# A fused two-layer block: half of the tokens' experts by gathered rows, half dense, in place of a quarter and three quarters

## The chip, the cores and the metric

One Trainium2 chip, one core. The metric is the device time of one execution in microseconds (us). The kernel before was timed three times: 2209.03, 2210.12 and 2216.78, so its median is 2210.12.

## The reference, cut to what matters

The program runs two transformer layers on 512 tokens of width 1024. The change touches the second half of the first layer, a product-key expert layer with 16384 experts of one row each:

```python
def block(xb):                                  # 128 tokens, width 1024
    q = (xb @ w_query).reshape(128, 8, 2, 128)
    s = einsum('chpd,hpnd->chpn', q, sub_keys)  # 8 heads, 2 halves, 128 keys
    top_s, top_i = top_k(s, 16)
    cand = top_s[:, :, 0, :, None] + top_s[:, :, 1, None, :]
    best_s, pos = top_k(cand, 16)               # 16 experts for each head
    idx = take(top_i[..0..] * 128 + top_i[..1..], pos)
    g = softmax(best_s)
    act = gelu(einsum('cd,chkd->chk', xb, expert_u[idx]))
    return einsum('chk,chkd->cd', g * act, expert_v[idx])
```

Each token thus uses 8 x 16 = 128 rows of `expert_u` and 128 rows of `expert_v`, of 4 KB each. Attention and a norm come before; the final norm, another attention and a dense feed-forward layer come behind.

## The kernel before, in words

All products on TensorE are done as three matmuls of split operands (`mm3`, lines 198 to 201): every weight tile is loaded by SP (line 93), copied to a rounded high part by ACT (line 111), and the low part is subtracted by VectorE, or by GpSimd where the stream says `lo=G` (line 112). `Stream` keeps 4 raw tiles of 128x512 in flight and 5 split ones.

The expert layer is done in two ways at once.

**Gathered:** for token block 0 (128 tokens on 128 partitions) the 128 chosen rows of `u` and the 128 of `v` are fetched by indirect DMAs from GpSimd's queue, one expert slot of all 128 tokens, 128 rows of 4 KB, at a time (`gather`, lines 1065 to 1078). VectorE forms each dot product with `hn` (line 1070), and adds each weighted `v` row to `acc` (line 1078). The row tiles are three (line 976), used in turn by `u` and `v`.

**Dense:** for blocks 1 to 3 (TD = 384 tokens) all 16384 experts are computed, 128 experts at a time: `u_side(b)` (24 matmuls of 384 columns, line 1029), gelu, a multiplication with the gates of the 128 experts (`weigh`), and `v_side` (3 token blocks x 2 halves x 3 matmuls of 512 columns into six PSUM banks, line 1055). The gate of every (expert, token) pair is built from the chosen indices by one-hot tiles on VectorE and matmuls on TensorE (`gate_hot`, `gate_sum`) for groups of 8 tokens, in three chunks of 38, 45 and 45 experts-rows, into a ring of 60 slots.

The order is: `query`, `level1`, `level2` for the 8 heads with all four blocks together (lines 939 to 948; the top-k runs on VectorE, with candidate sums and index selects partly on GpSimd); then the first chunk of gates (48 groups, lines 1096 to 1102); then the loop over the 128 dense expert blocks (lines 1115 to 1130), in which the other two chunks of gates are built in two stretches of blocks, and gathered units are handed out by a planned share for each block (`share`, `scale`, `due`). After block 120 the gathered block is finished with the residual and the final norm (lines 1132 to 1144); behind the loop the same is done for the other three blocks (lines 1179 to 1190).

GpSimd issues its instructions in order, so a gather that waits for a free row tile holds back the low parts and index selects that stand behind it; VectorE and TensorE are in order too. The order on an engine is made by the framework from priorities, and `issue_after` pins it.

Of the kernel before, what the change touches and what calls it, by code (L numbers as in the profile page):

```python
# [9 lines left out]
FT = mybir.dt.float32  # L10
# [10 lines left out]
P = 128  # L21
# [11 lines left out]
TD = S - P  # L33
CH = (38, 45, 45)
CW = max(CH)
RING = 60
# [11 lines left out]
RB = 1  # L48
ADA_E = 8
# [108 lines left out]
def body(ctx, tc, a):  # L158
# [622 lines left out]
    hA = pk.tile([P, 2, KD, S], FR, name="hA")  # L781
    hD = hA[:, :, :, P:]
    h0 = hA[:, :, :, :P]
    late["h0"] = h0
    hn = pk.tile([P, D], FT, name="hn")
    gw0 = pk.tile([P, P], FT, name="gw0")
    idx = pk.tile([P, P], I32, name="idx")
    iT = pk.tile([P, 2, TD], F16, name="iT", tag="iT")
    gp = pk.tile([P, TD, 2], F16, name="gp", tag="gp")
    ioth = pk.tile([P, P, 4], F16, name="ioth")  # L790
    with ExitStack() as s2:
        pn = pool(s2, "pn", 2)

        def norm2(b):
# [66 lines left out]
    def level1(m, top, tif):  # L861
        q = m % 2
# [11 lines left out]
        sc = pb.tile([P, NB, P], FT, name=f"scs{m}", tag="scs", bufs=2)  # L874
        A.activation(sc, p2, AF.Copy)
        ti = pb.tile([P, NB, 16], U32, name=f"tpi{m}", tag="tpi")
        for b in range(NB):
            V.max(out=top[:, b, q, 0:8], in_=sc[:, b])
            V.max_index(out=ti[:, b, 0:8], in_max=top[:, b, q, 0:8], in_values=sc[:, b])
            V.match_replace(out=sc[:, b], in_to_replace=top[:, b, q, 0:8], in_values=sc[:, b], imm_value=LOWEST)  # L880
            V.max(out=top[:, b, q, 8:16], in_=sc[:, b])
            V.max_index(out=ti[:, b, 8:16], in_max=top[:, b, q, 8:16], in_values=sc[:, b])
        A.activation(tif[:, :, q], ti, AF.Copy)

    def level2(h, top, tif):

        sh = [P, NB, 16]
        cand = pb.tile([P, NB, 80], FT, name=f"cand{h}", tag="cand")
        G.tensor_tensor(cand[:, :, 0:16], top[:, :, 0, 0:1].to_broadcast([P, NB, 16]), top[:, :, 1, :], op=OP.add)
        G.tensor_tensor(cand[:, :, 16:72].rearrange("p b (u w) -> p b u w", w=8),  # L890
                        top[:, :, 0, 1:8, None].to_broadcast([P, NB, 7, 8]),
                        top[:, :, 1, None, 0:8].to_broadcast([P, NB, 7, 8]), op=OP.add)
        G.tensor_tensor(cand[:, :, 72:80], top[:, :, 0, 8:16], top[:, :, 1, 0:1].to_broadcast([P, NB, 8]), op=OP.add)
        best = pb.tile([P, NB, 16], FT, name=f"best{h}", tag="best")
        pos = pb.tile([P, NB, 16], U32, name=f"pos{h}", tag="pos")
        for b in range(NB):
            V.max(out=best[:, b, 0:8], in_=cand[:, b])
            V.max_index(out=pos[:, b, 0:8], in_max=best[:, b, 0:8], in_values=cand[:, b])
            V.match_replace(out=cand[:, b], in_to_replace=best[:, b, 0:8], in_values=cand[:, b], imm_value=LOWEST)
            V.max(out=best[:, b, 8:16], in_=cand[:, b])  # L900
            V.max_index(out=pos[:, b, 8:16], in_max=best[:, b, 8:16], in_values=cand[:, b])
        ge = pb.tile([P, NB, 16], FT, name=f"ge{h}", tag="ge")
        V.tensor_tensor(ge, best, best[:, :, 0:1].to_broadcast(sh), op=OP.subtract)
        last["exp"] = A.activation(ge, ge, AF.Exp).ins

        i0 = pb.tile(sh, I32, name=f"i0{h}", tag="i0")
        V.tensor_scalar(i0, pos, 8.0, 0.0, op0=OP.subtract, op1=OP.max)
        ex = pb.tile(sh, FT, name=f"ex{h}", tag="ex")
        V.tensor_scalar(ex, pos, 72.0, 0.0, op0=OP.subtract, op1=OP.max)
        t1 = pb.tile(sh, FT, name=f"t1{h}", tag="t1")  # L910
        V.tensor_scalar(t1, pos, 16.0, -8.0, op0=OP.is_ge, op1=OP.mult)
        V.tensor_scalar(i0, i0, 3, None, op0=OP.arith_shift_right)
        V.tensor_add(t1, t1, pos)
        wi = pb.tile([P, 2, NB, 16], F16, name=f"wi{h}", tag="wi")
        V.tensor_add(wi[:, 0], i0, ex)
        V.scalar_tensor_tensor(t1, i0, -8.0, t1, op0=OP.mult, op1=OP.add)
        V.tensor_sub(wi[:, 1], t1, ex)
        hs = slice(h * 16, (h + 1) * 16)
        for q in range(2):

            for k0, n in ((0, 8), (8, 16)):
                eq = pb.tile([P, NB, 16, 8], F16, name=f"eq{h}_{q}_{k0}", tag="eq", bufs=5)[:, :, :n]
                V.tensor_tensor(eq, wi[:, q, :, None, k0:k0 + 8].to_broadcast([P, NB, n, 8]),
                                iotk[:, None, 0:n].to_broadcast([P, NB, n, 8]), op=OP.is_equal)
                G.tensor_tensor(eq, eq, tif[:, :, q, 0:n, None].to_broadcast([P, NB, n, 8]), op=OP.mult)
                eqs.append((ix[:, q, :, h * 16 + k0:h * 16 + k0 + 8], eq.rearrange("p b n k -> p b k n")))
        gs = pb.tile([P, NB], FT, name=f"gs{h}", tag="gs")
# [646 lines left out]
```

## Time and profile before

| | |
|---|---|
| runs, median (lowest, highest) | 2210.12 us (2209.03, 2216.78) |
| profiled execution, own time | 2222.11 us |
| its span | 2220.3 us |
| TensorE (PE) busy | 2102.8 us, 95% |
| VectorE (DVE) busy | 1624.1 us, 73% |
| ScalarE (ACT) busy | 954.2 us, 43% |
| GpSimd (POOL) busy | 618.3 us, 28% |
| DMA moved | 375.79 MB, 169 GB/s over the span |
| of which gathered rows' queue | 134.23 MB |

The span is that of the program on the core; the own time adds what lies around it. Matmuls overlap each other in the records, so a busy PE is not PE at its peak: the step from one matmul's start to the next tells its cost. Stretches of the span that belong to a stage are read with the view of windows: busy time of each engine in a stretch, then the granted clock as a share of full speed, the busy share of the 16 DMA engines and the GB/s moved.

### The profile page before, as it was taken

Reading aid. Unit: us, or ns where it says so; the run is one execution under the profiler, and the core shown is the slowest. Engines: PE = TensorE matmul, PEld = TensorE weight load, DVE = VectorE, ACT = ScalarE, POOL = GpSimd, SP = SyncE. Lnnn points to the kernel's source line nnn. Section 1 sums busy time; section 2 is a strip of 40 time slices with the busy share of each in tenths; the row PEclk is TensorE's granted clock in tenths of the full one; section 3 lists DMA queues with packets and bytes.
Section 4 is the critical chain, followed back from the end, with each engine's and each line's share of the span. In section 5 each row is a group of like instructions: output and inputs, shape, how many; then the busy total and the mean of one; then the engine's idle time right before and its main releaser. Section 6 shows DMA issues by size and latency. Waiting matters only on the chain.

```text
span 2220.3 us, 35038 instructions
## 1 busy us (share of the span) xinstructions
PE 2102.8 (95%) x12443; PEld 1771.4 (80%) x12443; DVE 1624.1 (73%) x3587; ACT 954.2 (43%) x1899; POOL 618.3 (28%) x553
## 2 busy tenths in 40 slices
PE   7999998888999999999999999999998999999999
PEld 5756787778888888888888888788887678888887
DVE  7779889997878997777799777777767865333322
ACT  4467342345435553333355433333353553333321
POOL 2245245564222113333312233333303420000000
PEclk9999999988999999999999999999999999999999
DMA  8515522231575558878855688888844221333332
GB/s 273 166 49 164 173 70 66 89 111 57 172 254 191 168 166 270 281 268 285 285 186 165 196 279 268 262 265 281 295 138 122 65 67 45 98 96 99 95 117 73
DMA packets 163634, 375.79 MB, mean 169 GB/s; under 512 B 18562, under 2 KB 22530, under 8 KB 163459
## 3 DMA queue, kind: packets, MB, share of 16 engines
q1 hardware_dynamic: 121058, 233.81, 31.6%
q0 software_dynamic: 36864, 134.23, 19.3%
q10 hardware_dynamic: 5536, 5.51, 0.9%
q8 instruction: 98, 1.61, 0.3%
q14 instruction: 78, 0.63, 0.1%
HBM read 366.66 MB, written 4.19 MB: 167 GB/s over the span
## 4 chain that ended last, share of the span: by engine, by line
PE 56%; DVE 16%; DMA 15%; issue 6%; ACT 4%; POOL 2%; ACTq 0%; SPq 0%; DVEq 0%; POOLq 0%
DMA vr<-in_v_dram,idx 7%; PE vac L200 4%; PE vac L201 4%; PE vac L199 4%; PE pA L199 4%; PE pA L200 4%; PE pA L201 3%; DMA wr<-in_uT_dram 3%; DMA ur<-in_u_dram,idx 3%; PE pd L201 2%; PE pd L200 2%; PE pd L199 2%; PE upp L201 2%; PE upp L199 2%; PE upp L200 2%
## 5 line engine op out<-in xcount | busy, mean ns | idle before, releaser
L111 ACT ACTIVATE wh<-wr 128x512 fp32r<-128x512 f32 x716 | 446.8, 631 | 760.4 <-DMA wr<-in_v_dram 162.1
L112 DVE TENSOR_TENSOR wl<-wr,wh 128x512 fp32r<-128x512 f32 x640 | 429.4, 695 | 286.4 <-ACT wh L111 270.2
L200 PE MATMUL vac<-wl,wwh 128*128 128x512 f32 x756 | 305.4, 404 | 32.7 <-DVE wl L112 32.3
L199 PE MATMUL pA<-hA,wh 128*128 128x384 f32 x928 | 318.1, 343 | 0.0
L201 PE MATMUL pA<-hA,wl 128*128 128x384 f32 x928 | 314.7, 339 | 0.0
L200 PE MATMUL pA<-hA,wh 128*128 128x384 f32 x928 | 313.9, 338 | 0.0
L199 PE MATMUL vac<-wh,wwh 128*128 128x512 f32 x756 | 304.3, 403 | 0.7 <-ACT wwh L1042 0.5
L201 PE MATMUL vac<-wh,wwl 128*128 128x512 f32 x756 | 299.5, 396 | 0.1
L1067 POOL DMA_INDIRECT ur<-in_u_dram,idx x128 | 160.5, 1254 | 383.3 <-DVE acc L1078 308.2
L1067 POOL DMA_INDIRECT vr<-in_v_dram,idx x128 | 155.3, 1213 | 338.2 <-DVE ur L1070 252.5
L200 PEld LDWEIGHTS vac<-wl,wwh 128*128 128x128 f32 x756 | 144.2, 191 | 73.5 <-DVE wl L112 49.2
L1078 DVE SCALAR_TENSOR_TENSOR acc<-vr,act,acc 128x1024 f32<-128x1024 f32 x127 | 162.7, 1281 | 46.7 <-DMA vr<-in_v_dram,idx 45.4
L1070 DVE SCALAR_TENSOR_TENSOR ur<-ur,hn 128x1024 f32<-128x1024 f32 x128 | 156.2, 1220 | 39.0 <-DMA ur<-in_u_dram,idx 39.0
L199 PEld LDWEIGHTS pA<-hA,wh 128*128 128x128 f32 x928 | 177.0, 191 | 4.1 <-ACT ga L1031 0.7
L200 PEld LDWEIGHTS pA<-hA,wh 128*128 128x128 f32 x928 | 177.0, 191 | 3.1
L201 PEld LDWEIGHTS pA<-hA,wl 128*128 128x128 f32 x928 | 176.6, 190 | 0.0
L201 PEld LDWEIGHTS vac<-wh,wwl 128*128 128x128 f32 x756 | 144.0, 190 | 30.1 <-DVE wwl L1043 0.8
L199 PEld LDWEIGHTS vac<-wh,wwh 128*128 128x128 f32 x756 | 144.1, 191 | 28.7 <-ACT wh L111 0.9
L112 POOL TENSOR_TENSOR wl<-wr,wh 128x512 fp32r<-128x512 f32 x76 | 101.9, 1352 | 74.6 <-ACT wh L111 71.7
L1042 ACT ACTIVATE wwh<-w 128x384 fp32r<-128x384 f32 x126 | 66.0, 524 | 117.2 <-DVE w L1035 115.0
L1008 PEld LDWEIGHTS <-oj 128*128 128x128 f16 x1152 | 83.2, 117 | 38.1 <-issue 16.4
L989 DVE TENSOR_TENSOR oj<-iT,ioth 128x1024 f16<-128x1024 f16 x144 | 106.0, 740 | 9.2 <-PE pG L1009 9.2
(697 smaller groups left out, 4319.7 us busy)
## 6 DMA issues: line engine op xcount, KB each, us to landing
wr<-in_uT_dram SPq DMA_DIRECT2D x256, 256.0 KB
wr<-in_v_dram SPq DMA_DIRECT2D x256, 256.0 KB
wa<-in_w_adaT_dram SPq DMA_DIRECT2D x48, 512.0 KB
wr<-in_w_gate_dram SPq DMA_DIRECT2D x44, 256.0 KB
wr<-in_w_up_dram SPq DMA_DIRECT2D x44, 256.0 KB
wr<-in_w_down_dram SPq DMA_DIRECT2D x44, 256.0 KB
wr<-in_w_in_dram SPq DMA_DIRECT2D x36, 256.0 KB
wr<-in_w_out_dram SPq DMA_DIRECT2D x32, 256.0 KB
```

The lines of the kernel that those rows point to most:

```text
L111: self.nc.scalar.activation(hi, raw, AF.Copy)
L112: (lo_eng or self.nc.vector).tensor_tensor(lo, raw, hi.bitcast(FT), op=OP.subtract)
L199: T.matmul(out, lh, rh, start=start, stop=False)
L200: T.matmul(out, lh, rl, start=False, stop=False)
L201: return T.matmul(out, ll, rh, start=False, stop=stop).ins
L989: V.tensor_tensor(out, iT[:, q, tt].rearrange("p (s t) -> p s t", t=4)[:, :, None].to_broadcast([P, GS // 4, w, 4]), ioth[:, None, j0:j0 + ...
L1008: T.matmul(pt[:, t, :n], oj[:, t // 4, :, t % 4], o[:, :, 1], start=True, stop=False)
L1042: A.activation(wh, w, AF.Copy)
L1067: G.indirect_dma_start(out=r, out_offset=None, in_=a[kind], in_offset=bass.IndirectOffsetOnAxis(ap=idx[:, j:j + 1], axis=0))
L1070: V.scalar_tensor_tensor(r, r, 1.0, hn, op0=OP.mult, op1=OP.mult, accum_out=act[:, j:j + 1])
L1078: V.scalar_tensor_tensor(acc, r, act[:, j:j + 1], acc, op0=OP.mult, op1=OP.add)
```

## The change

Blocks 0 and 1 are gathered now, blocks 2 and 3 dense (TD = 256).

- `u_side` has matmuls of 256 columns, `v_side` four accumulators in place of six. The gates are built in two chunks of 64 (64 groups of 8 tokens in place of 144); the ring has 74 slots.
- There are 512 gathers in place of 256. While the top-k runs there are 4 row tiles, later 8.
- The `v` rows are summed on TensorE: `actT` holds the weights with expert slots on partitions, `idxT` the indices transposed alike, so that one gather fetches the 128 experts of one token. Four tokens' rows are multiplied by 32-column tiles (`zc`, one column of weights in it), each into its own quarter of the 128 PSUM partitions, two halves of 512 columns.
- The top-k is a class. Block 0 runs through it beside the query matmuls (6 gathers and dots handed out behind each head, from the second head on), blocks 2 and 3 behind them (10 behind each head), with four of the early `u` blocks; block 1 in the first 8 of the dense loop's blocks. Scores wait in the ring, block 1's in the `acc` tiles. The softmax over the 16 chosen is done for all heads at once.
- In the first chunk of gates 24 units are handed out; in the dense loop what is left, evenly up to block 120.
- Block 0 is finished at block 100, block 1 at block 121, blocks 2 and 3 behind the loop.

The diff, cut to its core:

```diff
-TD = S - P
-CH = (38, 45, 45)
+NGB = 2
+TD = S - NGB * P
+CH = (64, 64)
-RING = 60
+RING = 74
+DOT_A, DOT_B = 6, 10
+ROWS = 4
+FEED_G, G_END, F_0 = 24, 121, 100
-U_TAIL = 6
+U_TAIL = 4
...
-        for o in ((slice(0, 256), slice(256, S)) if len(ms) > 1 else (ALL,)):
+        for o in (slice(0, 256), slice(256, S)):
             for m in ms:
-                lin(qps[m], w[m], KD, o, lambda k: hA[:, 0, k, o], lambda k: hA[:, 1, k, o])
+                lin(qps[m], w[m], KD, o, *hcol(o))
...
-        sc = pb.tile([P, NB, P], FT, name=f"scs{m}", tag="scs", bufs=2)
-        A.activation(sc, p2, AF.Copy)
+        A.activation(scores(m), p2, AF.Copy)
...
+    def gather(kind, b, j):
+        n = more.get("n", 0) % (2 * ROWS)
+        if n < ROWS:
+            r = pr.tile([P, D], FT, name=f"{kind}r{b}_{j}", tag="row")
+        else:
+            r = more["rows"][:, n - ROWS]
+        if more:
+            more["n"] += 1
+        i = idx[b] if kind == "u" else idxT[b]
+        G.indirect_dma_start(out=r, out_offset=None, in_=a[kind],
+                             in_offset=bass.IndirectOffsetOnAxis(ap=i[:, j:j + 1], axis=0))
+        rows[kind, b, j] = r
+    def dot(b, j):
+        r = rows.pop(("u", b, j))
+        V.scalar_tensor_tensor(r, r, 1.0, hn[b], op0=OP.mult, op1=OP.mult, accum_out=act[b][:, j:j + 1])
+    def feed(n):
+        for _ in range(n):
+            if not queue:
+                break
+            u = queue.pop(0)
+            gather(*u)
+            work.append(u)
+            while len(work) > (ROWS - 1 if not more else 2 * ROWS - 1 if work[0][0] == "u" else ROWS):
+                settle(*work.pop(0))
+    def values(b, q):
+        if q == 0:
+            gv[:] = [ps.tile([P, 512], FT, name=f"gv{b}{n}", tag=f"gv{n}") for n in range(2)]
+        z = zc[q % len(zc)]
+        A.activation(z[:, :, 31], actT[b][:, q::32], AF.Copy)
+        r = [rows.pop(("v", b, 32 * g + q)) for g in range(4)]
+        for n in range(2):
+            for g in range(4):
+                T.matmul(gv[n][32 * g:32 * g + 32], z[:, g, 31 - q:63 - q], r[g][:, n * 512:(n + 1) * 512],
+                         start=q == 0, stop=q == 31)
...
+    k0 = TopK(pb, "a", 1, lambda m: scores(m)[:, 0:1], ixg[0][:, :, None], gw0[0][:, None])
     for h in range(8):
+        k0.start()
+        score(2 * h)
+        k0.level1(2 * h)
+        if h:
+            k0.flush()
+            head_idx(k0, 0, h - 1)
+            queue += [("u", 0, (h - 1) * 16 + j) for j in range(16)]
+        score(2 * h + 1)
+        k0.level1(2 * h + 1)
+        k0.level2(h)
...
+        feed(DOT_A)
...
+    k2 = TopK(pb, "b", NB - NGB, lambda m: scores(m)[:, NGB:], ix, gw)
+    nu = iter(range(len(u_at), n_early))
+    for h in range(8):
+        k2.start()
+        k2.level1(2 * h)
+        k2.flush()
+        k2.level1(2 * h + 1)
+        feed(DOT_B // 2)
+        k2.level2(h)
+        feed(DOT_B - DOT_B // 2)
+        b = next(nu, None)
+        if b is not None:
+            u_early(b)
...
     for i in range(NG):
         gate_group(0, i)
...
+        feed((i + 1) * FEED_G // NG - i * FEED_G // NG)
...
         wts = weigh(b + 1)
-        due += share[b] * scale
-        while done < min(len(units), round(due)):
+        if b < 8:
+            k1.start()
+            k1.level1(2 * b)
+            k1.flush()
+            k1.level1(2 * b + 1)
+            k1.level2(b)
+        elif b == 8:
+            k1.flush()
+            k1.gates()
+            for h in range(8):
+                head_idx(k1, 1, h)
+            idx_rows(1, "pG")
+            queue += [("u", 1, j) for j in range(P)] + v_tokens(1)
+        left = len(queue) + (2 * P if b < 8 else 0)
+        n = 0 if b >= G_END else -(-left // (G_END - b))
+        with tc.issue_after(last["w"]):
+            feed(n)
+        if b == F_0:
+            mod_row(ps, "pA", gf, 40, "gf")
             with tc.issue_after(last["w"]):
-                gather(*units[done])
-            done += 1
+                finish(0, gains(), "0")
+        if b == G_END:
+            while work:
+                settle(*work.pop(0))
+            fg = gains()
+            with tc.issue_after(last["w"]):
+                finish(1, fg, "1")
```

## Rows read from the trace of the kernel before

**Rows 1.** Windows, by stage: us; PE, PEld, DVE, ACT, POOL busy; clock, DMA share, GB/s.
```profile
295.00:466.00 171.00, 148.09 (x750) 128.40 (x749) 162.62 (x926) 56.52 (x121) 97.20 (x103) 0.96 0.26 79
475.00:573.00 98.00, 86.60 (x1060) 80.63 (x1059) 81.23 (x141) 50.82 (x86) 45.32 (x37) 0.90 0.26 83
573.00:1603.00 1030.00, 994.63 (x6081) 870.75 (x6080) 822.01 (x1350) 443.43 (x858) 312.28 (x253) 0.99 0.73 241
...
1260.00:1600.00 340.00, 319.98 (x1566) 282.96 (x1565) 255.02 (x375) 125.76 (x226) 128.38 (x104) 0.98 0.82 273
```

**Rows 2.** Timeline of PE: start us, us, instruction; one dense block.
```profile
900.68 0.39 PE L199 MATMUL vac<-wh,wwh 128*128 128x512 f32 x1
...
904.80 0.33 PE L199 MATMUL pA<-hA,wh 128*128 128x384 f32 x1
...
908.99 0.39 PE L199 MATMUL vac<-wh,wwh 128*128 128x512 f32 x1
```

**Rows 3.** Waits, 1260 to 1600 us: engine line <- releaser: total us, times, longest.
```profile
POOL vr L1067 <- DVE ur L1070: 80.1, 22, 6.1
```

**Rows 4.** Timeline of PE: matmuls of 256 columns.
```profile
285.95 0.28 PE L199 MATMUL qp<-hA,wh 128*128 128x256 f32 x1
...
288.11 0.28 PE L199 MATMUL qp<-hA,wh 128*128 128x256 f32 x1
```

**Rows 5.** Timeline of DVE: part of one head's top-k, four blocks.
```profile
371.06 0.47 DVE L878 MAX8 top<-scs 128x8 f32<-128x128 f32 x2
...
375.75 0.36 DVE L897 MAX8 best<-cand 128x8 f32<-128x80 f32 x2
...
379.42 0.20 DVE L903 TENSOR_TENSOR ge<-best 128x64 f32<-128x64 f32 x1
...
380.82 2.49 DVE L923 TENSOR_TENSOR eq<-wi,iotk 128x512 f16<-128x512 f16 x3
```

**Rows 6.** Groups by line, whole span: count | busy us, mean ns | idle before.
```profile
L1067 POOL DMA_INDIRECT ur<-in_u_dram,idx x128 | 160.5, 1254 | 383.3 <-DVE acc L1078 308.2
```

**Rows 7.** Groups by line and shape, GpSimd, 295 to 466 us.
```profile
L112 POOL TENSOR_TENSOR wl<-wr,wh 128x512 fp32r<-128x512 f32 x47 | 60.0, 1289 | 36.3 <-ACT wh L111 36.1
```

**Rows 8.** Timeline of DVE where gates are built.
```profile
704.39 1.22 DVE L1070 SCALAR_TENSOR_TENSOR ur<-ur,hn 128x1024 f32<-128x1024 f32 x1
...
706.73 0.68 DVE L989 TENSOR_TENSOR oj<-iT,ioth 128x1024 f16<-128x1024 f16 x1
707.34 0.34 DVE L989 TENSOR_TENSOR oi<-iT,ioth 128x360 f16<-128x360 f16 x1
707.59 0.68 DVE L112 TENSOR_TENSOR wl<-wr,wh 128x512 fp32r<-128x512 f32 x1
708.19 0.53 DVE L996 TENSOR_TENSOR og<-oi,gp 128x360 f32<-128x360 f16 x1
708.64 0.68 DVE L112 TENSOR_TENSOR wl<-wr,wh 128x512 fp32r<-128x512 f32 x1
```

**Rows 9.** Windows in the dense loop, columns as rows 1.
```profile
1000.00:1020.00 20.00, 18.65 (x92) 16.16 (x91) 14.80 (x23) 7.18 (x13) 6.77 (x6) 1.00 0.89 304
1075.00:1080.00 5.00, 5.00 (x29) 4.79 (x28) 3.29 (x5) 1.32 (x3) 2.08 (x2) 1.00 0.99 372
```

**Rows 10.** Timeline of PE: f32 matmuls, 512 columns, and 128 columns by halves.
```profile
200.54 1.88 PE L269 MATMUL mlsc<-km,qm 128*128 128x512 f32 x4
...
1767.85 1.09 PE L329 MATMUL atpo<-atpT,vn 128*64 128x128 f32 x16
```

**Rows 11.** Chain in order of time, behind the dense loop.
```profile
1671.38 1.27 DVE n31t L229 x2
...
1682.87 0.45 PE n33pt L226 x4
```

**Rows 12.** Timeline of PE: 256 columns at the lower clock.
```profile
293.23 0.41 PE L200 MATMUL qp<-hA,wh 128*128 128x256 f32 x1
293.45 0.41 PE L201 MATMUL qp<-hA,wl 128*128 128x256 f32 x1
```

More of the change, by code (lines that the diff above doesn't have):

```diff
@@ L48 @@
 RB = 1
+FEED_G, G_END, F_0 = 24, 121, 100
+OGB = 3
 ADA_E = 8
@@ L883, in level1 @@
[L883 to L917, printed above, removed]
-        hs = slice(h * 16, (h + 1) * 16)
[L919 to L927, printed above, removed]
-        V.tensor_reduce(gs, ge, axis=AX.X, op=OP.add)
-        V.reciprocal(gs, gs)
-        V.tensor_tensor(gw[:, :, hs], ge, gs[:, :, None].to_broadcast(sh), op=OP.mult)
@@ new lines, in dot @@
+    def dot(b, j):
+        r = rows.pop(("u", b, j))
+        V.scalar_tensor_tensor(r, r, 1.0, hn[b], op0=OP.mult, op1=OP.mult, accum_out=act[b][:, j:j + 1])
+    work = []
+    def feed(n):
[17 more added lines that the diff above has]
+                         start=q == 0, stop=q == 31)
+        if q == 31:
+            for n in range(2):
+                A.activation(acc[b][:, n * 512:(n + 1) * 512], gv[n], AF.Copy)
@@ L943, in body @@
-        level1(2 * h, top, tif)
-        flush()
-        level1(2 * h + 1, top, tif)
-        level2(h, top, tif)
-        if h == 0:
-            back()
-    for b in range(len(u_at), len(u_at) + U_F):
+        k0.start()
[8 more added lines that the diff above has]
+        k0.level2(h)
+        if h == 0:
+            back(0)
@@ new lines, in body @@
+        feed(DOT_A)
+    k0.flush()
+    k0.gates()
+    head_idx(k0, 0, 7)
+    queue += [("u", 0, 7 * 16 + j) for j in range(16)]
+    back(1)
+    sc1 = acc[0].rearrange("p (m n) -> p m n", n=P), acc[1].rearrange("p (m n) -> p m n", n=P)
+    allsc = ring[:, 0:32].rearrange("p a t -> p (a t)").rearrange("p (m b n) -> p m b n", n=P, b=NB)
+    for i in range(2):
+        A.activation(sc1[i], allsc[:, 8 * i:8 * i + 8, 1], AF.Copy)
+    idx_rows(0, "ps")
+    more.update(rows=pk.tile([P, ROWS, D], FT, name="more", tag="hG"), n=0)
@@ L953, in body @@
-    V.tensor_copy(gw0, gw[:, 0])
+    k2.flush()
+    k2.gates()
     for q in (1, 0, 2):
         pt = ps.tile([P, 512], FT, name=f"ixT{q}", tag="ps")
-        for b in range(1, NB):
-            T.transpose(pt[:, (b - 1) * P:b * P], ix[:, q, b] if q < 2 else gw[:, b], ident)
+        for b in range(NB - NGB):
+            T.transpose(pt[:, b * P:(b + 1) * P], ix[:, q, b] if q < 2 else gw[:, b], ident)
         if q < 2:
@@ L964, in body @@
             V.tensor_tensor(gp[:, :, 0], gt, gp[:, :, 1], op=OP.subtract)
-    for b in range(len(u_at) + U_F, n_early):
-        u_early(b)
     s1.close()
@@ L975, in body @@
     pg = pool(s1, "pg", 2)
-    pr = pool(s1, "prow", 3)
-    ps = ps.then(pA=3, pG=3, rest=2)
-    pac = pool(s1, "pac")
-    act = pac.tile([P, P], FT, name="act")
-    acc = pac.tile([P, D], FT, name="acc")
-    starts = [sum(CH[:c]) for c in range(3)]
+    t = ps.tags["ps"]
+    ps = ps.then(pA=2, pG=2, gv0=1, gv1=1, rest=2)
+    starts = [sum(CH[:c]) for c in range(len(CH))]
     def gate_hot(c, g):
@@ L1046, in v_side @@
     def v_side(*v):
-        for t in range(3):
+        for t in range(NB - NGB):
             sl = slice(t * P, (t + 1) * P)
```

313 lines of the change are left out of this document (195 added, 118 removed).

## The prediction

> **What bounds the kernel now.** I read the windows by stage first [rows 1]. In the dense loop, 573 to 1603 us, TensorE is busy for 995 of 1030 us: that is the bound to look behind. In the query and top-k stage, 295 to 466 us, VectorE is busy for 163 of 171 us and bounds it; in the first gate stage, 475 to 573 us, VectorE (81) and TensorE (87) share it. The timeline of one dense block [rows 2] gives its price: 18 matmuls of 512 columns in 4.12 us (0.229 each) and 24 of 384 in 4.19 us (0.175 each), 8.31 us for a block. In the stretch from 1260 to 1600 us [rows 1] 104 gathers of 0.524 MB were issued while 273 GB/s moved: 92.8 MB, of which 54.5 are gathered, so 38.3 MB are dense, and at 1.049 MB for a block (u and v, 128x1024 floats each) that is 36.5 blocks of 9.3 us. So even now the transfers and the wait for the three row tiles (GpSimd waits 80 us of the 340 for a dot alone [rows 3]) take 1 us of each block beyond TensorE.
>
> **The dense loop after.** TensorE: 256-column matmuls step 0.12 us (18 steps in 2.16 [rows 4]), so u costs 24 x 0.12 = 2.9, v 12 x 0.229 = 2.7: 5.6 us. Weighted v rows come back to it: eight f32 matmuls for four gathers. One of 512 columns costs 0.47 (4 in 1.88), 128 columns thus about 0.118; in halves of the columns they step 0.068 [rows 10], 0.58 of that, so halves overlap. Quarters cost between 0.12 and 0.47 each; I take 0.58 x 0.47 = 0.27. With 3 gathers for a block, 6 matmuls: 1.6 us, at worst 2.8. TensorE needs 7.2 us (8.4 at worst).
>
> Transfers: heads 1 to 7 hand out 42 of block 0's u units, the next stage 80, the gate stage 24 (6 u, 18 v); 110 v units are left, with 256 of block 1 that is 366 over 121 blocks, 3.02 for each. A block moves 1.049 + 3.02 x 0.524 = 2.63 MB. That is now the bound, and its rate is the unknown that counts. Low end: 273 GB/s as in the stretch above, at a share of 0.82. High end: the fullest 5 us, 372 GB/s at 0.99 [rows 9]. I take 315: the fullest 20 us moved 304 at 0.89 with three row tiles [rows 9], and eight tiles take away most waits of [rows 3]; that share at 0.92 gives 315. One block then takes 8.36 us (9.64 at 273, 7.08 at 372).
>
> Two groups of blocks are held by VectorE. Steps [rows 8]: low part 0.60, oj 0.61, oi of 360 columns 0.25, og 0.45; by width, 512 columns give oi 0.36, og 0.64. The second chunk of gates falls in blocks 54 to 62, 3.56 groups each: 3.56 x 1.61 = 5.7, four low parts 2.4, weights 0.7, three dots at 1.22 are 3.7: 12.5 us, nine times 112. Blocks 0 to 7 carry block 1's top-k, 6.4 us a head (below), with two low parts and the weights: 8.3, with its waits on GpSimd 9; eight times 72. The other 104 blocks: 869. Block 0's early finish puts some 8 us of VectorE work, two table loads of ACT and 1 MB of loads on SP in one block: 8. Sum 1061 against 1030: **+31** (+165 at 273 GB/s, -102 at 372).
>
> **Query and top-k.** For four blocks one half-head of level 1 takes 4.69 us and level 2 3.67 [rows 5]; nine short instructions take 1.4; the stage's 21.4 us a head (171 / 8) leave 6.9 for the eq products and sums, which go by elements. One block: 2.34 + 0.92 + 1.4 + 1.7 = 6.4 us. Two blocks: 4.69 + 1.84 + 1.4 + 3.5 = 11.4.
>
> Beside the queries, one head of block 0 now needs: VectorE 6.4 + 6 dots x 1.22 = 13.7; TensorE 96 x 0.12 + scores 0.9 = 12.4, and 2.9 for each of six early u blocks in heads 4 to 7; GpSimd four low parts x 1.29 [rows 7], six gathers x 1.25 [rows 6] and some 1.5 of selects (my estimate: few elements in seven short instructions) = 14.2, and 2.6 for each u block. With four row tiles a gather in GpSimd's queue waits for a dot, and the low parts of the next query weights stand behind it: I add 2. Heads: 12.5, 3 x 16, 17, 20, 20, 17 and 5 for the transposes back: 140 against 171, **-31** (-45 to -15).
>
> Then comes a new stage that is not hidden: blocks 2 and 3 need 11.4 us a head and 10 dots 12.2, 23.6 us on VectorE, eight times **+189** (177 if the short instructions shrink too, 205 with a us or two of waiting for candidate sums behind gathers). Its cover on TensorE is four early u blocks, 12 us; no dense work can be pulled forward, as the gates need every head's indices. Copies of scores, the second transposes and the softmax between the stages: **+5**.
>
> **First gates.** 32 groups x (0.61 + 0.36), two thirds of the og at 0.64, six dots: 44 + 7 = 52 us of VectorE; at the stage's ratio of span to busy, 98 / 81, 63 against 98: **-35** (-45 to -20); the ten u blocks that stood beside it are gone.
>
> **Tail.** Seven blocks without gathers cost 2.7 us less each: -19. One block fewer is normed behind the loop; from block 1's transposes to block 3's the chain takes 11.5 us for two [rows 11], I take -9. **-28** (-40 to -15).
>
> **Sum.** -31 + 5 + 189 - 35 + 31 - 28 = **+131**. The profiled execution's own time is 2222.11, so 2353 by its measure; it stands 12 above the median, so 2341.
>
> **A price that only a page gives.** The Trainium skill, "DMA: Bandwidth & Descriptors", section "Specifications", puts HBM's limit for one core at about 358 GB/s. The 372 of [rows 9] stands above it, so for short stretches the trace doesn't bear it out. By that limit a block takes 7.35 us, the loop 957 and the whole 2237, an estimate.
>
> **The rivals.**
> - Rate stays near 273 to 290 GB/s: the row tiles were not what held it back. For it: 340 us at 273. Against: the waits of [rows 3]. From +206 to +265: 2416 to 2475. Chance 0.20.
> - Rate of 340 to 355 once both queues always hold requests: at 340 a block takes 7.74, loop 997, total +67: 2277; at 355 2243. For it: 5 us at 372. Chance 0.19.
> - Faster: one mechanism, the transfer rate of the 104 blocks. At 372 GB/s the sum is -2: that is the point from which it decides, with the stages as above. With the query, second top-k and gate stages all at their low ends (36 less) it needs only 354 to break even, and at 372 gives -38, so 2172. Against: it must hold for 800 us what one 5 us window showed. Chance 0.07; between, within 0.5% (11 us, about what a measurement of this kernel can tell), 0.04.
> - The clock. TensorE now waits in every block. Where its clock fell, 256-column matmuls step 0.22 us [rows 12], not 0.12; a dense block would take about 5.3 + 5.5 + 1.6 = 12.4 us, and if all did, +420. Against: the stretch with waits for transfers keeps a granted clock of 0.98 [rows 1]. Chance 0.05, at some 2445 if a quarter of the blocks fall. The rule behind it is in the Trainium skill, "TensorE: Matmul & The Clock Gate", section "Why this matters for your kernels": idle gaps between bursts bring the low level back. At that level the sum would be the one just given, and the row speaks against it.
> - The quarters don't overlap: 8.4 us a block on TensorE against 8.36, some 10 us over the v blocks; inside the range.
>
> **Numbers.** The forecast itself, 2300 to 2400, has 0.45. The range, 2245 to 2460, takes in the second rival and most of the first. Faster by over 0.5% 0.07, within 0.04, slower 0.89.
>
> **What would show it.** A stage of some 190 us behind the queries with VectorE near 100%, TensorE near idle and DMA under 250 GB/s; dense blocks of 8.4 us with a DMA share over 0.9 and TensorE waiting for weights, not VectorE; 12 us for blocks with gates. Wrong: a loop well under 1000 us, or a top-k stage that hides behind dense work.

## The result, and the profile after

The changed kernel takes 2345.23 us (median of four runs, 2340.61 to 2352.85) against 2212.42 for the kernel before: 1.060 times as long, 95% interval 1.057 to 1.064. It is **slower** by 133 us, as forecast. Its profiled execution took 2352.85 us with a span of 2350.6, which is 130.3 us more than the span of before; the stages below are compared by these two spans.

First the windows by stage, of before and of after, with the columns of [rows 1]. The marks are the last top-k instruction, the first matmul of the dense loop and the last one: the loop here holds all 128 blocks.

Kernel before (its first gates are in [rows 1]):

```profile
295.00:475.00 180.00, 153.84 (x777) 134.15 (x777) 170.53 (x936) 63.62 (x136) 105.41 (x110) 0.94 0.27 82
...
573.00:1663.00 1090.00, 1052.94 (x6377) 921.76 (x6376) 860.30 (x1419) 476.66 (x919) 317.24 (x257) 0.99 0.72 237
1663.00:2220.00 557.00, 540.36 (x2731) 439.88 (x2729) 269.92 (x512) 201.77 (x367) 55.44 (x52) 0.98 0.28 87
```

Kernel after:

```profile
295.00:647.00 352.00, 159.38 (x1081) 153.49 (x1079) 312.94 (x1130) 65.95 (x150) 285.84 (x288) 0.69 0.69 224
647.00:721.00 74.00, 48.53 (x581) 28.35 (x581) 65.39 (x124) 35.21 (x42) 41.94 (x34) 0.70 0.57 182
721.00:1792.00 1071.00, 943.45 (x5863) 702.82 (x5864) 673.69 (x1438) 442.12 (x907) 444.41 (x422) 0.95 0.85 301
1792.00:2350.00 558.00, 542.57 (x2716) 441.05 (x2715) 268.20 (x504) 199.45 (x362) 52.80 (x50) 0.98 0.27 87
```

The whole loss is in the first line: queries and top-k go from 180 to 352 us (+172), with VectorE at 313 of 352. The gates give back 24 (98 to 74), the loop 19 (1090 to 1071), and what is behind it is equal. +172 - 24 - 19 + 1 = +130.

The same view inside the loop of after: v rows of block 0; u rows of block 1; the second chunk of gates; u again; v rows of block 1.

```profile
815.00:1000.00 185.00, 178.65 (x1173) 133.59 (x1173) 88.08 (x173) 79.29 (x163) 80.22 (x80) 0.99 0.94 347
1000.00:1155.00 155.00, 124.41 (x717) 100.61 (x716) 118.86 (x210) 60.51 (x116) 70.37 (x53) 0.93 0.88 308
1155.00:1295.00 140.00, 97.23 (x811) 81.68 (x811) 104.52 (x194) 58.26 (x118) 38.00 (x27) 0.80 0.53 173
1295.00:1445.00 150.00, 123.11 (x670) 96.96 (x670) 120.12 (x217) 58.49 (x115) 72.61 (x55) 0.95 0.92 323
1445.00:1755.00 310.00, 294.62 (x1918) 217.26 (x1921) 141.30 (x249) 131.22 (x275) 118.73 (x119) 0.99 0.93 340
```

Where v rows come in, 340 to 347 GB/s move at a share of 0.93 to 0.94, against 273 at 0.82 in [rows 1]. Where u rows come in it is 308 to 323, and in the gate blocks, 140 us for nine of them, only 173, at a share of 0.53: there the queues are far from full.

Single blocks are counted from one `wwl` (the low part of a block's weights, one for each block) to another on VectorE's timeline of after: those of blocks 14, 36, 54, 63 and 121, counted from 0.

```profile
829.42 0.42 DVE L1193 TENSOR_TENSOR wwl<-w,wwh 128x256 fp32r<-128x256 f32 x1
...
993.77 0.43 DVE L1193 TENSOR_TENSOR wwl<-w,wwh 128x256 fp32r<-128x256 f32 x1 [0.48 <-issue]
...
1146.84 0.41 DVE L1193 TENSOR_TENSOR wwl<-w,wwh 128x256 fp32r<-128x256 f32 x1
...
1287.40 0.43 DVE L1193 TENSOR_TENSOR wwl<-w,wwh 128x256 fp32r<-128x256 f32 x1 [0.45 <-ACT wwh L1192]
...
1748.83 0.43 DVE L1193 TENSOR_TENSOR wwl<-w,wwh 128x256 fp32r<-128x256 f32 x1 [0.48 <-ACT wwh L1192]
```

The first two are 22 blocks apart, 7.47 us each; the third and fourth are the nine gate blocks, 15.6 each; without these, the 98 blocks from the first row to the last take 317.4 + 461.4 = 778.9 us, 7.95 each (8.36 was forecast).

### The profile page after: what moved, and what is told of

It reads as the page before. It is cut to its first block, busy times and chain, and to the rows that moved or that the text cites. A ratio compares the mean times of both kernels' runs of the same rounds, so it can differ in the third digit from the quotient of the medians.

```text
span 2350.6 us, 34412 instructions
## 1 busy us (share of the span) xinstructions
PE 1963.2 (84%) x11764; PEld 1520.8 (65%) x11764; DVE 1565.7 (67%) x3773; ACT 904.2 (38%) x1852; POOL 920.7 (39%) x895
## 4 chain that ended last, share of the span: by engine, by line
PE 41%; DMA 23%; DVE 18%; issue 6%; ACT 6%; POOL 4%; SPq 0%; ACTq 0%; DVEq 0%; POOLq 0%
DMA wr<-in_v_dram 12%; DMA wr<-in_uT_dram 8%; PE gv L1022 4%; DVE ur L998 3%; ACT wh L115 3%; DVE wl L116 3%; DVE more L998 2%; PE pd L205 2%; PE pd L203 2%; PE pd L204 2%; PE upp L205 2%; PE upp L203 2%; PE upp L204 2%; PE gatep L204 2%; PE gatep L203 2%
## 5 line engine op out<-in xcount | busy, mean ns | idle before, releaser
L203 PE MATMUL pA<-hD,wh 128*128 128x256 f32 x944 | 282.1, 299 | 42.3 <-ACT ga L1181 41.5
L205 PE MATMUL pA<-hD,wl 128*128 128x256 f32 x944 | 275.2, 292 | 6.6 <-DVE wl L116 6.1
L204 PE MATMUL pA<-hD,wh 128*128 128x256 f32 x944 | 272.2, 288 | 0.0
L203 PEld LDWEIGHTS pA<-hD,wh 128*128 128x128 f32 x944 | 185.5, 197 | 105.8 <-ACT ga L1181 71.0
L992 POOL DMA_INDIRECT more<-in_v_dram,idxT x128 | 132.5, 1035 | 171.3 <-PE gv L1022 131.9
L992 POOL DMA_INDIRECT more<-in_u_dram,idx x106 | 139.3, 1314 | 144.1 <-DVE more L998 114.2
L205 PEld LDWEIGHTS pA<-hD,wl 128*128 128x128 f32 x944 | 186.1, 197 | 13.4 <-DVE wl L116 9.2
L992 POOL DMA_INDIRECT vr<-in_v_dram,idxT x128 | 133.8, 1045 | 151.6 <-PE gv L1022 115.1
L204 PEld LDWEIGHTS pA<-hD,wh 128*128 128x128 f32 x944 | 185.8, 197 | 2.7 <-issue 1.3
L1022 PE MATMUL gv<-vr,zc 128*32 128x512 f32 x512 | 144.8, 612 | 3.4 <-DMA vr<-in_v_dram,idxT 2.4
L1022 PE MATMUL gv<-more,zc 128*32 128x512 f32 x512 | 139.7, 612 | 2.3 <-DMA more<-in_v_dram,idxT 2.3
L998 DVE SCALAR_TENSOR_TENSOR more<-more,hn 128x1024 f32<-128x1024 f32 x106 | 128.3, 1238 | 6.4 <-DMA more<-in_u_dram,idx 6.4
```

Source lines behind the costliest of these rows:

```text
L203: T.matmul(out, lh, rh, start=start, stop=False)
L204: T.matmul(out, lh, rl, start=False, stop=False)
L205: return T.matmul(out, ll, rh, start=False, stop=stop).ins
L992: G.indirect_dma_start(out=r, out_offset=None, in_=a[kind], in_offset=bass.IndirectOffsetOnAxis(ap=i[:, j:j + 1], axis=0))
L998: V.scalar_tensor_tensor(r, r, 1.0, hn[b], op0=OP.mult, op1=OP.mult, accum_out=act[b][:, j:j + 1])
L1022: T.matmul(gv[n][32 * g:32 * g + 32], z[:, g, 31 - q:63 - q], r[g][:, n * 512:(n + 1) * 512], start=q == 0, stop=q == 31)
```

## The experiments

Eleven kernels were run. Two questions lead: is the loop held by its transfers, and is the stage ahead of it held by VectorE? Times are compared with 2345 for the kernel after and with the runs of the kernel before on the same chip.

**1. Half of the loop's gathers.**

```diff
+        if more.get("loop"):
+            more["loop"] += 1
+            if more["loop"] % 2:
+                rows[kind, b, j] = late["grow"]
+                return
...
-        rows[kind, b, j] = r
+        rows[kind, b, j] = late["grow"] = r
...
+    more["loop"] = 1
```

> In the dense loop every second gather is left out and the row tile of the gather before is used twice; dots, weighted sums and dense work all stay. So some 183 x 0.524 = 96 MB of the loop's 316 MB (1037 us at 305 GB/s) are not moved. Theory T (the loop is held by its transfers): the loop falls until TensorE and the gate blocks hold it: 104 blocks of about 6.3 us, 9 gate blocks of 12.5, 8 blocks with the top-k of 9, some 840 to 930 us against 1037, and the whole 2180 to 2270. Rival R1 (each block is held by a chain of waits of its own, not by bytes: four weight tiles in flight, or a row tile's turn): the loop loses less than 30 us, the whole stays at 2315 or more. Rival R2 (TensorE holds it): no change.

Measured: 2249.76 us, 95 less. Its loop, by windows:

```profile
717.00:1690.00 973.00, 885.28 (x5860) 689.67 (x5861) 667.57 (x1439) 450.53 (x906) 229.49 (x239) 0.97 0.71 233
```

So the gathers do hold the loop back, but not far: the whole is in theory T's band, the loop's 973 us not in its 840 to 930. What stands close below is on VectorE's timeline, blocks of the v stretch:

```profile
909.10 0.42 DVE L1198 TENSOR_TENSOR wwl<-w,wwh 128x256 fp32r<-128x256 f32 x1 [0.48 <-ACT wwh L1197]
916.77 0.43 DVE L1198 TENSOR_TENSOR wwl<-w,wwh 128x256 fp32r<-128x256 f32 x1 [0.48 <-ACT wwh L1197]
922.39 0.43 DVE L1198 TENSOR_TENSOR wwl<-w,wwh 128x256 fp32r<-128x256 f32 x1 [0.48 <-ACT wwh L1197]
```

A block with a sum of four v rows takes 7.67 us, one without takes 5.62: the eight quarter matmuls cost 2.05, or 0.26 each, and three sums in four blocks make TensorE's price 7.16 a block. The prediction had 0.27 and 7.2. The kernel after, at 7.47, stands 0.3 us above that floor. 183 units left out (a unit is one gather with what reads it) gave 98 us of the loop, 0.54 each: a third of the 1.54 us that 0.524 MB take at 340 GB/s. Counted by `wwl`, only 8 of the 98 lie in the v stretch of block 0, and 17 in the nine gate blocks, where the queues were far from full, so it is not the bytes alone that they free.

**2. Dots of block 0 cut to 8 columns.**

```diff
-        V.scalar_tensor_tensor(r, r, 1.0, hn[b], op0=OP.mult, op1=OP.mult, accum_out=act[b][:, j:j + 1])
+        if b:
+            V.scalar_tensor_tensor(r, r, 1.0, hn[b], op0=OP.mult, op1=OP.mult, accum_out=act[b][:, j:j + 1])
+        else:
+            V.scalar_tensor_tensor(r[:, 0:8], r[:, 0:8], 1.0, hn[b][:, 0:8], op0=OP.mult, op1=OP.mult, accum_out=act[b][:, j:j + 1])
```

> Block 0's 128 dot products are cut to 8 of 1024 columns, its gathers all stay (left out: nearly all of the sums over columns for block 0). Theory V (between the queries and the gates VectorE holds the time, and dots are 178 of its 312 busy us there): that stretch, 352 us, falls to where its 79 MB at about 340 GB/s take over, some 230 to 270 us, and the whole to 2230 to 2270. Rival (the stretch is held by the landing of gathers with four row tiles, or by GpSimd's queue): the stretch loses under 40 us, the whole stays above 2305.

Measured: 2285.71 us, 60 less; between the two bands. The windows of the stretch and of its end:

```profile
295.00:594.00 299.00, 143.64 (x1050) 138.15 (x1049) 192.11 (x1127) 62.39 (x145) 211.74 (x280) 0.74 0.76 260
...
500.00:594.00 94.00, 3.50 (x13) 2.06 (x12) 55.20 (x371) 9.14 (x25) 60.37 (x85) 0.50 0.80 288
```

VectorE held the stretch (312.9 of 352 us busy with the dots, 192 of 299 without), but only 53 us above the next limit: with the dots nearly free, the last 94 us run at 288 GB/s with VectorE 59% busy. There 31 of VectorE's 39 idle us are waits for landing rows (total us, times, longest):

```profile
DVE ur L1001 <- DMA ur<-in_u_dram,idx: 16.7, 14, 3.6
DVE more L1001 <- DMA more<-in_u_dram,idx: 14.6, 12, 2.1
```

The tile `more` holds the second four row tiles: the kernel uses them from the end of block 0's top-k on, so beside the searches of blocks 2 and 3 there are eight and not, as the section on the change has it, four. GpSimd waits under 1 us there for a tile, but 20 us for VectorE's indices. Whether the landing of rows or the order of these two queues is that next limit, no run took apart.

**3. More v units in the stage of the first gates.**

```diff
-FEED_G, G_END, F_0 = 24, 121, 100
+FEED_G, G_END, F_0 = 48, 121, 100
```

> 24 more of block 0's v units are handed out in the stage of the first gates (48 in place of 24) and as many fewer in the loop. Theory T: the loop loses 24 x 0.524 MB, 12.6 MB at 330 GB/s, 38 us; the gate stage, 72 us at a DMA share of 0.57, takes most of them beside its VectorE work and grows by 5 to 20; net 15 to 33 us faster, 2312 to 2330. Rival (the loop is not held by bytes, or the gate stage has no room): 0 to 15 us slower.

Measured: 2344.78 us, ratio to before 1.058 (1.052 to 1.064): no change, and my expectation missed. The gate stage grew from 74 to 91 us while its rate rose from 182 to 279 GB/s, and the loop gave back 12; the stretch ahead of the gates, which the edit leaves alone, came out 8 shorter (windows, columns as above):

```profile
639.00:730.00 91.00, 70.93 (x671) 32.29 (x672) 70.75 (x146) 36.46 (x47) 67.70 (x62) 0.84 0.84 279
730.00:1789.00 1059.00, 921.09 (x5774) 697.90 (x5773) 668.16 (x1417) 438.82 (x901) 418.64 (x394) 0.95 0.83 294
```

0.5 us for a unit taken out of the loop, as in the first run, and 0.7 for one put into the gates. The loop is not a pipe of bytes alone.

**4. v rows summed on VectorE, as before.**

```diff
-            if j // 32 == 3:
-                values(b, j % 32)
+            r = rows.pop(("v", b, j))
+            if j == 0:
+                V.tensor_scalar(vsum[b], r, act[b][:, 0:1], None, op0=OP.mult)
+            else:
+                V.scalar_tensor_tensor(vsum[b], r, act[b][:, j:j + 1], vsum[b], op0=OP.mult, op1=OP.add)
...
-            while len(work) > (ROWS - 1 if not more else 2 * ROWS - 1 if work[0][0] == "u" else ROWS):
+            while len(work) > (ROWS - 1 if not more else 2 * ROWS - 1):
...
```

> The weighted v rows are summed as in the kernel before: gathered by expert slot and added up on VectorE, 256 steps of about 1.2 us, no quarter matmuls, and the bytes stay the same. Theory T (bytes hold the loop): VectorE goes from 645 to about 950 busy us of the loop's 1037 but still hides, with 7.0 us a block against 7.8: 2340 to 2375. Rival (VectorE would have held the loop, so the sum on TensorE is what keeps the change from being worse): loop 80 to 150 us longer, 2425 to 2495.

Measured: 2429.3 us, ratio 1.094 (1.086 to 1.102): the rival's band. Summing on TensorE is worth 84 us of this design, so it is not what made the change slow.

```profile
722.00:825.00 103.00, 55.34 (x163) 40.87 (x164) 100.87 (x391) 21.65 (x48) 63.49 (x84) 0.70 0.61 202
830.00:1000.00 170.00, 133.99 (x722) 115.76 (x723) 135.40 (x182) 64.61 (x124) 84.02 (x60) 0.90 0.87 307
```

The edit also lets seven v units wait in the queue, not four. Where block 1's top-k runs (first line) VectorE is at 98% and the rate falls to 202 GB/s. In the v stretch (second line) no engine and no queue is full: VectorE 80%, share 0.87, a block at 8.5 us in place of 7.47. Every row tile there waits for an add in VectorE's queue behind low parts and weights; that may be the reason, but no run took it apart.

**5. Four row tiles in the loop in place of eight.**

```diff
-        if n < ROWS:
+        if n < ROWS or late.get("r4"):
...
-            while len(work) > (ROWS - 1 if not more else 2 * ROWS - 1 if work[0][0] == "u" else ROWS):
+            while work and len(work) > (ROWS - 1 if not more else (3 if late.get("r4") else 7) if work[0][0] == "u" else 0 if late.get("r4") else ROWS):
...
+    late["r4"] = True
```

> The dense loop has four row tiles in place of eight (a gather waits for the tile four before it). Theory T2 (the loop is held about equally by TensorE, 7.2 us a block where v rows are summed, and by the landing of rows; eight tiles keep transfers and TensorE from waiting for each other): the rate falls back towards the 273 GB/s of the kernel before, the loop grows from 1070 by 80 to 170 us, the whole 2425 to 2515. Rival (the rate doesn't hang on tiles in flight, only on bytes): 2330 to 2365.

Measured: 2471.26 us, 126 more, in the middle of the band of the theory. The v stretch by windows, and the longest of its waits (total us, times, longest):

```profile
815.00:1000.00 185.00, 176.56 (x939) 111.24 (x939) 75.29 (x164) 66.83 (x137) 61.07 (x69) 1.00 0.84 282
```

```profile
POOL vr L992 <- PE gv L1022: 121.7, 29, 10.6
```

From 830 to 1030 us, gathers stand for 122 of 200 us behind the sum that reads their tile, and the rate falls from 347 to 282 GB/s, a v block from 7.47 to 9.05 us. The u blocks ahead of the gates hardly move (8.32 and 8.24, 17 from block 37 on). So it takes more than four tiles to move v rows at 340 to 347 GB/s. A sum reads four tiles at once, so with four no gather can run beside it, and the edit also issues each sum right behind its fourth gather, not four gathers later: the run shows what the second four tiles are worth to these sums, not a rate for each tile.

**6. The kernel before with a fourth row tile.**

```diff
-    pr = pool(s1, "prow", 3)
+    pr = pool(s1, "prow", 4)
...
-        xn = (pr.tile([P, D], FT, name="xn31", tag="row"), acc, pf.tile([P, D], FT, name="xn33"))[b - 1]
+        xn = acc if b == 2 else pr.tile([P, D], FT, name=f"xn3{b}", tag="row")
```

> The kernel before with a fourth row tile (its last normed row takes the fourth tile, so that it fits). Prediction's reading of rows 3 (three row tiles hold back the dense loop of before, GpSimd waits 80 us of 340 for one): 10 to 50 us faster than before, ratio 0.977 to 0.995. Rival (TensorE, 995 busy of 1030 us, holds that loop whatever the tiles): within 6 us of before.

Measured: 2178.22 us, ratio 0.984 (0.981 to 0.988). **This beats both kernels**, by 36 us and 167 us. The window that answers to the last line of [rows 1], 104 gathers in 340 us there too, and all 128 blocks:

```profile
1222.00:1562.00 340.00, 334.80 (x1717) 300.35 (x1717) 268.75 (x395) 134.43 (x246) 139.28 (x104) 1.00 0.85 286
...
567.00:1621.00 1054.00, 1042.00 (x6381) 919.60 (x6382) 862.75 (x1423) 476.19 (x921) 335.48 (x256) 1.00 0.73 244
```

TensorE goes from 320 to 335 of 340 us and the loop from 1090 to 1054: the waits of [rows 3] did cost something, and TensorE, 98% busy, is now the likely bound of that design.

**7. No units beside the top-k of blocks 2 and 3.**

```diff
-DOT_A, DOT_B = 6, 10
+DOT_A, DOT_B = 6, 0
```

> No units are handed out beside the top-k of blocks 2 and 3; 80 gathers and dots go to the dense loop. Theory T2 (that stage is held by VectorE, where a dot costs 1.3 to 1.6 us; a unit in the loop costs 0.5 us by the run with half the gathers, up to 1.5 by bytes at 340 GB/s): the stretch from the queries to the gates falls from 352 by 85 to 115 us, the loop grows by 45 to 120: 2280 to 2375, middle 2320. Rival (bytes alone hold the loop, 80 x 1.55 = 124 us, and the stage falls only to the landing of its own transfers): 2365 to 2400.

Measured: 2335.15 us, ratio 1.054 (1.050 to 1.058), 10 less than after. By windows:

```profile
295.00:534.00 239.00, 145.53 (x1025) 140.13 (x1023) 218.74 (x969) 60.68 (x141) 168.56 (x209) 0.80 0.53 167
...
607.00:1777.00 1170.00, 965.67 (x5929) 734.82 (x5929) 752.09 (x1592) 446.26 (x915) 553.97 (x503) 0.90 0.87 313
```

The stretch lost 113 us, 1.4 for each unit and its dot, and the loop gained 99, 1.24 each. Two windows inside this loop show what the moved units met there:

```profile
607.00:720.00 113.00, 58.44 (x178) 44.31 (x178) 111.40 (x451) 25.86 (x54) 75.48 (x93) 0.68 0.69 228
...
830.00:1020.00 190.00, 183.55 (x1226) 130.73 (x1228) 82.00 (x139) 75.48 (x162) 93.65 (x95) 1.00 1.02 392
```

Counted by `wwl`, the first ten blocks, with block 1's top-k and 40 of the moved dots, take 38 us more than in the kernel after, and VectorE is busy for 111 of 113 us (first line): that part of the price is VectorE's. In the v stretch (second line) the queues are full, at 392 GB/s and a share of 1.02, and the 22 blocks from block 14 on take 26 us more. So a unit more cost 1.24 us in the loop and a unit less (the first and third runs) gave half a microsecond, but the two were not paid at the same place.

**8 and 9. Weights ahead of the gate sums,** in the kernel after and in the sixth kernel. The profile of after had shown a hole in every gate block, on VectorE's timeline and in the waits of 1155 to 1295 us:

```profile
1225.40 0.43 DVE L1193 TENSOR_TENSOR wwl<-w,wwh 128x256 fp32r<-128x256 f32 x1 [4.83 <-ACT wwh L1192]
```

```profile
ACT ring L1154 <- PE pG L1151: 42.1, 19, 4.3
DVE wwl L1193 <- ACT wwh L1192: 30.6, 10, 4.8
```

```diff
+        early = weigh(b + 1) if b in build else None
         v_side((b, *wts, [ws.get(("v", b, n)) for n in range(2)]))
         while hot:
             gate_sum(*hot.pop(0))
-        wts = weigh(b + 1)
+        wts = early or weigh(b + 1)
```

> In the nine blocks that build the second chunk of gates, the next block's weights are formed ahead of this block's v matmuls and gate sums instead of behind them. Theory G (there VectorE stands still 3 to 5 us a block, because ScalarE's high part of the weights waits behind its copies of the gate sums, and three dots wait behind the low part): the blocks fall from 15.5 to 12 to 13.5 us, 18 to 30 us in all, the whole 2312 to 2330. Rival (those blocks are held by VectorE's own work of 12.5 us and the gate sums' one bank, and the stall only moves): within 8 us of 2345.

> The kernel before with a fourth row tile and the same move of the weights in its two stretches of gate building. There a block takes 10 to 11.5 us against 8.3 of dense matmuls, TensorE has the gate sums besides. Theory G: 25 such blocks gain 0.3 to 1 us each, 2153 to 2171. Rival (TensorE holds those blocks): within 5 us of 2178.

Measured: 2332.51 us, ratio 1.052 (1.047 to 1.056), 13 less than after; and 2180.95 us, ratio 0.984 (0.979 to 0.989), nothing beside the sixth run's 2178. The nine gate blocks of the eighth kernel by windows:

```profile
1132.00:1245.00 113.00, 85.19 (x751) 70.91 (x750) 100.20 (x185) 56.73 (x111) 42.60 (x30) 0.89 0.71 234
```

They take some 113 us in place of 141, VectorE 89% busy: 28 us, as theory G said, and the prediction's 112 to a microsecond. But half of it is given back, so that the time lies between the two bands: the 19 blocks from block 63 on take 8.5 us each, not 8.1, and the 40 ahead of the gates 6 us more in all. Why is not shown; the gate blocks left no bytes behind, since 113 us at 234 GB/s are 26 MB and 140 at 173 are 24. In the design of before there was nothing to gain, as the rival has it, for which TensorE holds its gate blocks.

**10. Half of the quarter matmuls.**

```diff
-        for n in range(2):
+        for n in range(1):
             for g in range(4):
...
-                A.activation(acc[b][:, n * 512:(n + 1) * 512], gv[n], AF.Copy)
+                A.activation(acc[b][:, n * 512:(n + 1) * 512], gv[0], AF.Copy)
```

> Only the first 512 columns of the v rows are summed on TensorE (left out: the second half of the weighted sums; it is filled with the first), so a group of four rows costs four quarter matmuls in place of eight; all gathers stay. 64 groups at 2.05 us (blocks with a group take 7.7 us, without one 5.6, where half of the gathers are left out) lose about 1.03 each, some 62 of them in the loop. Theory T2 (bytes and TensorE stand close together where v rows are summed: 7.2 us a block by TensorE, 7.6 to 7.8 measured): 10 to 30 us faster, 2315 to 2335. Rival B (bytes alone): within 6 us of 2345. Rival P (TensorE alone): 55 to 65 us faster, 2280 to 2290.

Measured: 2325.6 us, ratio 1.051 (1.047 to 1.055), 20 less: the number of T2, but not its place. On VectorE's timeline the v stretch of block 0 has:

```profile
813.26 0.42 DVE L1193 TENSOR_TENSOR wwl<-w,wwh 128x256 fp32r<-128x256 f32 x1
...
977.68 0.43 DVE L1193 TENSOR_TENSOR wwl<-w,wwh 128x256 fp32r<-128x256 f32 x1 [0.48 <-ACT wwh L1192]
```

22 blocks of 7.47 us, the same as in the kernel after, although TensorE needs 0.8 us less for each. So TensorE does not hold that stretch. Neither does the top rate of the queues: they moved 347 GB/s in it, and 392 over 190 us in the 7th kernel, by which a block's 2.63 MB would take 6.7 us. What the kernel after shows there is gathers that wait for a sum to free their tiles, 85 of the 170 us from 830 to 1000, although with shorter sums the stretch is no quicker:

```profile
POOL more L992 <- PE gv L1022: 43.2, 9, 12.9
POOL vr L992 <- PE gv L1022: 41.7, 8, 10.7
```

What sets the 7.47 us stays open. The 20 us are in small pieces elsewhere (8 in the first 14 blocks, 5 in the gate blocks, which have no such sums, 5 in block 1's v stretch), and their cause stays open too.

**11. The top-k of blocks 2 and 3 kept behind block 0's.**

```diff
+    gate_exp = last["exp"]
     for h in range(8):
+      with tc.issue_after(gate_exp):
...
```

> The top-k of blocks 2 and 3 is kept behind block 0's, where the prediction had it, instead of partly among the queries. Theory S (VectorE's work is the same, its holes beside the queries are lost): the queries' stretch ends at some 140 to 155 us instead of 191, what is behind it grows to 190 to 215, together 340 to 365 against 352; the whole 2335 to 2360. Rival (the pulling forward hides much of that work): together 380 or more, the whole above 2372.

Measured: 2347.21 us, ratio 1.060 (1.057 to 1.062), no difference. VectorE's instructions on `topb`, the searches of blocks 2 and 3, by windows (us, VectorE busy, clock, share, GB/s), first of after, then of this kernel:

```profile
295.00:486.00 191.00, 18.08 (x96) 0.82 0.66 208
486.00:623.00 137.00, 25.19 (x160) 0.54 0.73 246
```

```profile
295.00:350.00 55.00, 8.58 (x40) 0.98 0.64 201
...
486.00:540.00 54.00, 13.82 (x88) 0.56 0.61 200
540.00:646.00 106.00, 19.50 (x128) 0.50 0.71 236
```

In the kernel after, 96 of 256 of them were drawn forward among the queries; here 40 still were, all by 350 us. The first gates begin at 646 or 647 us either way, with VectorE busy for 310 or 313 us of the stretch: its sum of work decides, not its order. The whole is theory S's, but not the split: the queries' part still ends near 486 us, 191 long, and not after 140 to 155.

## Why the prediction was right

Forecast +131 us against the profiled execution, measured +130; 2341 against 2345 by medians. That is closer than its terms were, and luck: their errors of +9, +11, -31 and +10 cancel. In the cut of the windows above (the loop with its last blocks, so +31 - 19 = +12 forecast for it, and -9 behind it):

| term | forecast | measured |
|---|---|---|
| queries, copies and top-k | -31 + 5 + 189 = +163 | +172 |
| first gates | -35 | -24 |
| dense loop, all blocks | +12 | -19 |
| behind the loop | -9 | +1 |
| sum | +131 | +130 |

- **Top-k stage: right in kind and size, wrong in its split.** The forecast had 140 us of queries and 189 of a bare stage behind them; measured are 191 and 161. The framework drew searches forward, which shortens the bare part and, by the 11th run, costs and gives nothing in all. But that is not what made the queries long: with 40 searches there in place of 96 they still took 191. The forecast had 42 dots there at 1.22 us, 51 in all; VectorE's group from 295 to 486 us (count, busy us, mean ns, idle before) has 50 that took 81:

```profile
L998 DVE SCALAR_TENSOR_TENSOR ur<-ur,hn 128x1024 f32<-128x1024 f32 x50 | 81.1, 1623 | 19.8 <-DMA ur<-in_u_dram,idx 19.6
```

  Their median is 1.23 us and the longest 4.33, so a few are held up, in a part where GpSimd forms 44 low parts; by what, no run shows. The signs named beforehand came (VectorE near 100%, TensorE near idle, under 250 GB/s), in the same columns:

```profile
486.00:647.00 161.00, 14.62 (x80) 12.48 (x79) 153.42 (x552) 15.27 (x38) 129.15 (x129) 0.53 0.73 243
```

  That VectorE holds it is shown by the 2nd and 7th runs. What was not seen: the next limit stands only 53 us behind, with the dots nearly free (2nd run).
- **Dense loop: rate underrated, mechanism right in part.** "I take 315" was the step that failed. The v stretches moved 340 to 347 GB/s, and the 98 plain blocks took 7.95 us, not 8.36: 40 us less, or 48 with the 8 that the forecast had besides for block 0's early finish, which falls among them. The fullest 20 us of before [rows 9] were taken as the bound's neighbour; with eight tiles its 304 was no ceiling. That gathers and their tiles hold the loop back is shown by the 1st and 5th runs. That each block is its bytes over one rate is not: half of the gathers gave a third of their bytes' time, and the same eight tiles moved 392 GB/s in the 7th kernel, where more rows were asked for.
- **Gate blocks: 28 us too low.** The 112 counted VectorE's work alone. The profile after shows VectorE standing 3 to 5 us in such a block, since ScalarE's high part of the weights waits behind its copies of the gate sums. The 8th run takes that away and comes to 113. This error and the one in the rate cancelled in part: -48 + 28, 14 less in the first 14 blocks and 2 more in the last ones make the loop's -31 to a microsecond.
- **Quarter matmuls: 0.27 forecast, 0.26 measured, by two errors.** The rows of the sum (16 records for eight matmuls) show that an f32 matmul leaves two records. The four records of [rows 10] are thus two matmuls, as line 269 has them, so the "0.47 for one of 512 columns" was half a matmul, and a whole one costs 0.94. Four quarters take 0.43 to 0.45 us for a record of each, as long as one record alone, so they overlap fully and not by the 0.58 of the halves. On PE's timeline one whole sum of the first run, then part of one of after:

```profile
909.63 1.92 PE L1027 MATMUL gv<-vr,zc 128*32 128x512 f32 x16
```

```profile
902.78 0.62 PE L1022 MATMUL gv<-vr,zc 128*32 128x512 f32 x2
902.79 0.62 PE L1022 MATMUL gv<-more,zc 128*32 128x512 f32 x2
903.23 0.60 PE L1022 MATMUL gv<-vr,zc 128*32 128x512 f32 x2
```

Four records start within 0.02 us and the next four 0.45 us later. The Trainium skill, "TensorEngine Tiling (Array Packing)", section "Performance Considerations", gives fourfold column tiling for a weight tile of 32 columns; the trace agrees, 0.45 us for four against 0.47 for one.

- **Gates and tail: both too hopeful by 10.** In the gates VectorE is busy 65 of 74 us where the forecast had 52 of 63: the one-hot tiles `oj` and `oi` last 0.82 and 0.55 us on the mean, where the sum took their steps in the loop of before, 0.61 and 0.36 [rows 8] (`oj` itself lasts 0.68 there). The first gates of before had the row to take: `oj` lasts 0.84 in them. VectorE's groups of 647 to 721 us in after, then of 475 to 573 us in before (count, busy us, mean ns, idle before):

```profile
L1131 DVE TENSOR_TENSOR oj<-iT,ioth 128x1024 f16<-128x1024 f16 x32 | 26.1, 819 | 4.7 <-PE pG L1151 3.7 <-remote 1.1
L1131 DVE TENSOR_TENSOR oi<-iT,ioth 128x512 f16<-128x512 f16 x32 | 17.4, 548 | 0.0
```

```profile
L989 DVE TENSOR_TENSOR oj<-iT,ioth 128x1024 f16<-128x1024 f16 x50 | 41.7, 844 | 9.2 <-PE pG L1009 9.2
```

  Behind the loop one block fewer to norm gave nothing (558 against 557 us): the -9 taken from [rows 11] did not come, and no run asked what took its place.

**The rivals.** The first, a rate that stays at 273 to 290, is what the 5th run makes by taking four tiles away: 282 GB/s in the v stretch and 2471 us, at the upper end of its 2416 to 2475. That the tiles decide was, for the v rows, the right reason against it. The quicker rate of the rival on the other side was reached in v stretches alone; u blocks at 308 to 323 GB/s and the gate blocks at 173 kept the mean at 301. The clock fell to 0.80 in the gate blocks and 0.53 in the bare top-k stage, where TensorE waits, and stayed at 0.99 where v rows move: no time like that rival's came of it.

## What to carry to other kernels

Price a change by the stage that it makes bare: the dense loop got 19 us shorter and yet the kernel 133 longer, because the top-k of two blocks and 80 dots, for which nothing else was ready on TensorE, stood alone on VectorE. When a loop gathers rows, count the tiles in flight first: a fourth tile for the old kernel was worth 36 us, more than twice what the best repair of the new one gave. And a price per unit measured in one direction does not hold in the other: a unit left out of this loop gave half a microsecond, a unit put in cost 1.24, over a third of it in blocks that VectorE held.

## What was not expected of the hardware

- With eight row tiles the DMA queues moved 347 and 340 GB/s over 185 and 310 us, and in the 7th kernel 392 over 190 us, at a share of 1.02. The prediction's page-only price used a limit of 358; the Trainium skill, "Perfetto Trace Analysis", section "Roofline", says that this is a share for two cores at work and that one alone may pull more. The trace agrees with that page, with 392.
- In the v stretch of this design the rate was 282 GB/s with four row tiles and 347 with eight (5th run). In the kernel before it was 273 with three [rows 1] and 286 with four (6th run), but there TensorE was 98% busy, so that the 286 need not be the most that four tiles give.
